# Later norm vectors: weights scaled on ScalarE, summed over k on GpSimd, partitions added once on TensorE

## The chip, the cores and the metric

The kernel runs on one core of one Trainium2 chip. The metric is device time in microseconds of one launch, the median of several runs. Besides, one execution was taken by the hardware profiler; its rows are what the prediction rests on. A core has five engines with a queue each: TensorE (PE in the rows, its weight loads PEld), VectorE (DVE), ScalarE (ACT), GpSimd (POOL) and SyncE (SP), which here issues the weight transfers.

## The reference

Two transformer layers on 512 tokens of width 1024, in float32. Each layer first makes six vectors of length 1024 out of one conditioning vector `c`; they scale, shift and gate the two halves of the layer. Cut to what matters:

```python
c_act = jax.nn.silu(c)                                  # [1, 1024]
for i in range(DEPTH):                                  # 2 layers
    mod = c_act @ ada_w[i] + ada_b[i]                   # [1, 6144], ada_w[i] is [1024, 6144]
    sh1, sc1, g1, sh2, sc2, g2 = jnp.split(mod[:, None, :], 6, axis=-1)
    h = _rmsnorm(x, norm_g[i, 0]) * (1.0 + sc1) + sh1
    mix = diff_attention(h, ...) if i % 2 == 0 else nsa_attention(h, ...)
    x = x + g1 * mix
    h = _rmsnorm(x, norm_g[i, 1]) * (1.0 + sc2) + sh2
    x = x + g2 * hier_moe(h, ...)                       # 32 experts, 2 of them for each token
return _rmsnorm(x, final_g)
```

## The kernel before

The product of `c_act` with `ada_w` (25 MB per layer) is done in blocks. Block (l, b) is two of the six vectors of layer l, 2048 columns of `ada_w`: b = 0 is sh1 and sc1, b = 1 is g1 and sh2, b = 2 is sc2 and g2. Block (0, 0) is needed at once and is made by `ada_first`; the other five, the later ones, by `ada_block`, a generator that is advanced in steps between other work.

A weight matrix has its 1024 rows laid out as 128 partitions by KC = 8 values of k. For each k, `ada_steps` multiplies the column `csil[:, k]` (silu of c, copied to 32 columns) with four groups of 512 columns, each into 32 partitions of one PSUM bank `acc`, so that the four land in four column groups of TensorE. The bank is added up over the eight k, then VectorE adds the bias (`nc.vector.tensor_tensor(row, acc, row, op=OP.add)`, line 243), the sc vectors get 1 + and the norm weight, and the four rows are stored to DRAM, from where later stages read them.

Weights stream through two units of 16 KB per partition, `ring[0]` and `ring[1]`, taken in turn by `unit()`. A block takes four units, two k each. Each unit is loaded in four pieces of 512 KB on SyncE's queue by `piece`, which lets a piece start only when the third one before it has landed and when its area of the ring has been read. The same two units also hold the weights of the projections (`w_in`, `w_out`), so blocks and projections follow one another there.

PSUM banks come from one pool with three names: four banks `mm` (projections, `ada` blocks, part of layer 1's scores), two `tr` (transposes), two `sc` (scores). A projection `dense` holds all four `mm` banks, one for each block of 128 rows, over its eight k; for each k, ScalarE and VectorE split 128x512 weights into two parts `wh` and `wl` (lines 369 and 370, four buffers each), and TensorE does three products for each row block.

The order of the work is written out by hand and then laid on the engines by the framework's scheduler, which takes instructions in the order of the program where they are ready:

```python
for w in "v0 h0 q1 a8 h1 h2 q2 a8 h3 v1 h4 q3 a8 h5".split():   # layer 0
```

Here q and v are projection units, h is an attention head, and a8 is eight steps, one whole block: (0,1), (0,2), (1,0). Behind a q unit come four rounds of evacuation: ScalarE copies the bank to `qkt`, GpSimd rotates it (`rope_to`, lines 324 to 330), TensorE transposes it, ScalarE and VectorE write it as two parts. Heads 6 and 7 and the output projection follow. In layer 1, `nsa_block` does two halves of eight scores for each of eight (group, row block) pairs and calls `do(ada_rest, 2)` once in each half, so blocks (1,1) and (1,2) are done in the first four pairs. In each half, GpSimd scales the first of four heads' weights `Pt`, VectorE the other three (line 1254), before TensorE transposes them.

Of the kernel before, what the change touches and what calls it, by code (L numbers as in the profile page):

```python
# [11 lines left out]
F32 = mybir.dt.float32  # L12
# [4 lines left out]
AF = mybir.ActivationFunctionType  # L17
OP = mybir.AluOpType
# [4 lines left out]
P = 128  # L23
# [3 lines left out]
KC = D // P  # L27
# [54 lines left out]
def tile_kernel(ctx, tc, x, c, positions, ada_w, ada_b, norm_g, final_g, diff_w_in, diff_w_out,  # L82
# [3 lines left out]
    nc = tc.nc  # L86
    pinned = set()

    def pin(i, engine):

        return tc.keep_in_program_order(i) if engine in pinned else i

    def mm(*a, **k):
        return pin(nc.tensor.matmul(*a, **k), "PE")  # L94
# [9 lines left out]
    cst = ctx.enter_context(tc.tile_pool(name="cst", bufs=1))  # L104
# [4 lines left out]
    def bank(tag):  # L109
        return ps.tile([P, 512], F32, name="b_" + tag, tag=tag, bufs={"mm": 4, "tr": 2, "sc": 2}[tag])  # L110
# [4 lines left out]
    def unit():  # L115
        t = ring[ring_at[0] % len(ring)]
        ring_at[0] += 1
        return t
# [3 lines left out]
    def piece(dst, src, paced=DEPTH_Q, after=None):  # L122


        i = nc.sync.dma_start(dst, src)
        if after is not None:
            tc.add_manual_dep(i.ins, after.ins.name,
                              mybir.DependencyInfo(mybir.DependencyClass.Sync, mybir.DependencyReason.DATA),
                              reason="behind the rows that the experts gather")
        if paced and len(stream) >= paced:  # L130
            tc.add_manual_dep(i.ins, stream[-paced].ins.name,
                              mybir.DependencyInfo(mybir.DependencyClass.Sync, mybir.DependencyReason.DATA),
                              reason="paced weight stream")
        stream.append(i)

    def wload(dst, src):
        h = dst.shape[-1] // 2
        if len(dst.shape) == 2:
            parts = [(dst[:, 0:h], src[:, 0:h]), (dst[:, h:], src[:, h:])]
        else:  # L140
            k = dst.shape[1] // 2
            parts = [(dst[:, 0:k], src[:, 0:k]), (dst[:, k:], src[:, k:])]
        for p in parts:
            piece(*p)
# [37 lines left out]

    ccol = cst.tile([P, KC], F32, name="ccol")
    nc.scalar.dma_start(ccol, c.rearrange("b (p k) -> (b p) k", k=KC))
    csil = cst.tile([P, KC], F32, name="csil")
    nc.scalar.activation(csil, ccol, AF.Silu)  # L186
    mod_d = [[dram.tile([4, 512], F32, name=f"mod{l}_{b}") for b in range(3)] for l in range(DEPTH)]

    def ada_steps(acc, l, b):

        for k in range(KC):
            if k % 2 == 0:
                w = unit()
                for kk in range(2):
                    wload(w[:, kk * 2048:(kk + 1) * 2048],
                          ada_w[l].rearrange("(p k) n -> p k n", k=KC)[:, k + kk, b * 2048:(b + 1) * 2048])
            lhsT = csil[:, k:k + 1].to_broadcast([P, 32])
            for g in range(4):
                c0 = k % 2 * 2048 + g * 512
                mm(acc[32 * g:32 * g + 32, :], lhsT, w[:, c0:c0 + 512], start=(k == 0), stop=(k == KC - 1),  # L200
                   skip_group_check=True)
            yield
# [24 lines left out]
        nc.vector.tensor_tensor(sh, cv[:, 0, :], bcol[:, 0, :], op=OP.add)  # L227
        return A, sh

    def ada_block(l, b):  # L230

        row = bcp.tile([P, D], F32, name="bc")
        row, gv = row[:, 0:512], row[:, 512:1024]
        lo = 64 if b == 0 else 0
        src = ada_b[l, b * 2048:(b + 1) * 2048]
        nc.scalar.dma_start(row, bass.AP(tensor=src.tensor, offset=src.offset, ap=[[512, 4], [0, 32], [1, 512]]))
        if b != 1:
            src = norm_g[l, 0 if b == 0 else 1]
            nc.scalar.dma_start(gv[lo:lo + 64], bass.AP(tensor=src.tensor, offset=src.offset,
                                                       ap=[[512, 2], [0, 32], [1, 512]]))  # L240
        acc = bank("mm")
        yield from ada_steps(acc, l, b)
        nc.vector.tensor_tensor(row, acc, row, op=OP.add)
        if b != 1:
            nc.vector.scalar_tensor_tensor(row[lo:lo + 64], row[lo:lo + 64], 1.0, gv[lo:lo + 64],
                                           op0=OP.add, op1=OP.mult)
        nc.scalar.dma_start(mod_d[l][b], row[0:P:32, :])
# [31 lines left out]
    with tc.tile_pool(name="rope", bufs=1) as rpool:  # L279
# [3 lines left out]
        kk = rpool.tile([P, NT, 8], F32, name="kk")  # L283
# [66 lines left out]
    def modulate(pool, tag, xk, k, Ac, shc, hi, lo):  # L350

        h = pool.tile([P, S], F32, name="h", tag=tag[0], bufs=tag[1])
        if k % 2:
            nc.scalar.activation(h, xk, AF.Identity, scale=Ac[:, k:k + 1], bias=shc[:, k:k + 1])
            nc.scalar.activation(hi[:, k, :], h, AF.Copy)
        else:
            nc.scalar.activation(hi[:, k, :], xk, AF.Identity, scale=Ac[:, k:k + 1], bias=shc[:, k:k + 1])
            nc.vector.tensor_scalar(h, xk, Ac[:, k:k + 1], shc[:, k:k + 1], op0=OP.mult, op1=OP.add)
        nc.vector.tensor_tensor(lo[:, k, :], h, hi[:, k, :].bitcast(F32), op=OP.subtract)
# [104 lines left out]
    m = main.enter_context(tc.tile_pool(name="main0", bufs=1))  # L464
    qkv_stack = ExitStack()
    qp = qkv_stack.enter_context(tc.tile_pool(name="qkv0", bufs=1, side="right"))
# [152 lines left out]
                    nc.vector.tensor_tensor(xs[:, t0 + u, qq], xs[:, t0 + u, qq], tmp, op=OP.add)  # L619

    qk_unit(0, lambda k: modulate(qp, ("wh", 4), xT[k // 4][:, k % 4, :], k, Ac, shc, hi, lo))
    ada0 = itertools.chain(ada_block(0, 1), ada_block(0, 2), ada_block(1, 0))
    for w in "v0 h0 q1 a8 h1 h2 q2 a8 h3 v1 h4 q3 a8 h5".split():
        {"v": v_unit, "q": qk_unit, "h": diff_head, "a": lambda n: do(ada0, n)}[w[0]](int(w[1:]))
    do(ada0)
# [382 lines left out]
    g = open_moe(0)  # L1008
# [14 lines left out]
    qp = qkv_stack.enter_context(tc.tile_pool(name="qkv1", bufs=1, side="right"))  # L1023
# [14 lines left out]
    w = unit().rearrange("p (k n) -> p k n", k=KC)  # L1038
# [6 lines left out]
    m = main.enter_context(tc.tile_pool(name="main1", bufs=1))  # L1045
# [73 lines left out]
    w = unit()[:, 0:KC * 304].rearrange("p (k n) -> p k n", k=KC)  # L1119
# [10 lines left out]
    b = bank("tr")  # L1130
# [26 lines left out]
    for cc in range(16):  # L1157
        for z, (blk, w1) in enumerate(rows):
            mm(hb[64 * z:64 * z + 64, 0:HID], blk[:, cc].rearrange("p g n -> p (g n)"), w1[cc // 8][:, cc % 8],
               start=(cc == 0), stop=(cc == 15), skip_group_check=True)  # L1160
# [7 lines left out]
    m1, m = m, main.enter_context(tc.tile_pool(name="main1b", bufs=1))  # L1168
# [6 lines left out]
    b = bank("tr")  # L1175
# [4 lines left out]
    b = bank("mm")  # L1180
# [12 lines left out]
    b = bank("mm")  # L1193
# [9 lines left out]
    def nsa_block(gi, i):  # L1203
# [65 lines left out]
        for st in range(2):  # L1269
            for hh in range(4):  # L1270
# [4 lines left out]

    ew = Experts(1, [("g", 0, 0), ("g", 0, 1), ("g", 2, 0), ("g", 1, 0), ("g", 1, 1), ("g", 2, 1), ("d", 0, 0), ("d", 1, 0), ("d", 2, 0),
                     ("d", 3, 0)])
    ada_rest = itertools.chain(ada_block(1, 1), ada_block(1, 2))
    w_o = nsa_w_out[0].rearrange("(g s h d) n -> g s d h n", g=2, s=2, h=4)

    def load_wo(w, q):
# [16 lines left out]
    g = open_moe(1)  # L1298
# [44 lines left out]
```

## Time and profile before

| | us |
|---|---|
| median of three runs | 1371.77 |
| lowest and highest | 1371.35, 1374.61 |
| the profiled execution | 1373.53 |
| its span, first to last instruction | 1371.7 |
| TensorE busy | 1267.9 |
| VectorE busy | 752.7 |
| ScalarE busy | 557.4 |
| GpSimd busy | 178.4 |

The profile gives the time in which an engine had an instruction in work as busy. Matmuls overlap one another in TensorE's pipeline, so its busy time is the time covered by at least one. A float32 matmul of two passes has two records. The granted clock is the share of TensorE's full clock of 2.4 GHz.

### The profile page before, as it was taken

The page shows a single profiled execution, that of the slowest core. Times are in us where ns is not written, and L with a number is a line of the kernel's source. Part 1 is how long each engine was busy: PE and PEld are TensorE (multiplying, and loading weights), DVE is VectorE, ACT ScalarE, POOL GpSimd, SP SyncE. Part 2 cuts the span into 40 slices and gives each one's busy share as a digit, 9 for nine tenths or more (in the row PEclk, how much of TensorE's full clock was granted, in tenths as well). Part 3 has the DMA queues.
Part 4 walks back from the last instruction along what each step waited for, and adds up shares of the span by engine and source line. Part 5 has one row for each costly group of instructions (what it writes and reads, how often), then busy time and mean ns, then how long its engine had stood idle before and what let it go on. Part 6 is the DMA issues. An engine that isn't in the chain of part 4 may idle for free.

```text
span 1371.7 us, 18259 instructions
## 1 busy us (share of the span) xinstructions
PE 1267.9 (92%) x6431; PEld 762.7 (56%) x6431; DVE 752.7 (55%) x1671; ACT 557.4 (41%) x1332; POOL 178.4 (13%) x304
## 2 busy tenths in 40 slices
PE   4899999989969999999799799999999599999995
PEld 0587668657734444444688554556558544444442
DVE  2444756586525555556654455657645426555557
ACT  2443644455423332222554444655644143332222
POOL 0021120212210000000142111112120200000001
PEclk7899999989969999999999899999999699999998
DMA  7722855486759999994432174510054579999971
GB/s 252 233 95 75 287 179 192 135 296 197 253 169 365 400 402 408 408 408 154 128 109 92 62 261 151 142 63 1 17 190 138 150 285 380 396 408 408 407 279 62
DMA packets 104607, 309.84 MB, mean 226 GB/s; under 512 B 13888, under 2 KB 27680, under 8 KB 104500
## 3 DMA queue, kind: packets, MB, share of 16 engines
q1 hardware_dynamic: 93920, 288.59, 58.3%
q0 software_dynamic: 6304, 12.96, 2.8%
q10 hardware_dynamic: 4276, 6.96, 1.7%
q8 instruction: 55, 0.90, 0.3%
q14 instruction: 52, 0.43, 0.1%
HBM read 310.52 MB, written 6.34 MB: 231 GB/s over the span
## 4 chain that ended last, share of the span: by engine, by line
PE 45%; DVE 2%; issue 2%; ACT 1%; DMA 1%; POOL 1%; ACTq 0%; POOLq 0%; DVEq 0%
PE b_mm L94 31%; PE b_sc L94 8%; PE b_tr L97 6%; DMA xg<-xr_d,toks 1%; DVE nm L397 0%; DVE xs L919 0%; DVE y L911 0%; ACT slot L398 0%; DVE yl L382 0%; DVE otmp L618 0%; ACT yh L381 0%; DVE slot L1254 0%; POOL rs L179 0%; DVE blk L1149 0%; ACTq L1129 0%
## 5 line engine op out<-in xcount | busy, mean ns | idle before, releaser
L94 PE MATMUL b_mm<-slot,xT 128*64 128x512 f32 x640 | 187.8, 608 | 2.3 <-ACT xT L868 2.0
L94 PE MATMUL b_mm<-ring,xT 128*64 128x512 f32 x384 | 126.6, 592 | 0.0
L94 PE MATMUL b_mm<-wh,h_hi 128*128 128x512 f32 (+1 forms) x320 | 116.5, 395 | 7.2 <-ACT wh L369 5.5
L94 PE MATMUL b_mm<-wl,h_hi 128*128 128x512 f32 (+1 forms) x320 | 122.2, 391 | 0.7 <-DVE wl L370 0.6
L94 PE MATMUL b_mm<-wh,h_lo 128*128 128x512 f32 (+1 forms) x320 | 120.5, 388 | 0.0
L94 PEld LDWEIGHTS b_mm<-slot,xT 128*64 128x64 f32 x640 | 60.0, 141 | 93.5 <-issue 86.4
L883 DVE TENSOR_TENSOR ac<-b_mm,sl 128x256 f32<-128x256 f32 x32 | 20.0, 625 | 159.8 <-ACT sl L881 159.8
L868 ACT ACTIVATE xT<-b_tr,col_sh,col_A 128x128 f32<-128x128 f32 x256 | 93.0, 468 | 2.5 <-PE b_tr L97 0.5
L919 DVE TENSOR_TENSOR xs<-xs,b_mm 128x512 f32<-128x512 f32 x128 | 86.4, 675 | 2.8 <-PE b_mm L94 2.8
L94 PE MATMUL b_mm<-ring,csil 128*32 128x512 f32 x384 | 78.6, 668 | 9.7 <-ACT csil L186 4.8
L919 DVE TENSOR_TENSOR xs<-xs,b_sc 128x512 f32<-128x512 f32 x128 | 86.5, 676 | 0.3 <-PE b_sc L94 0.3
L848 POOL DMA_INDIRECT xg<-xr_d,toks x32 | 32.4, 1012 | 358.7 <-DVE xn L855 321.4
L881 ACT ACTIVATE sl<-b_mm 128x256 f32<-128x256 f32 x32 | 12.3, 384 | 157.6 <-PE b_mm L94 147.9
L94 PE MATMUL b_sc<-slot,slot 128*128 128x128 f32 (+3 forms) x232 | 72.8, 389 | 3.8 <-ACT slot L398 1.3
L370 DVE TENSOR_TENSOR wl<-ring,wh 128x512 fp32r<-128x512 f32 (+1 forms) x80 | 53.2, 673 | 39.0 <-ACT wh L369 37.4
L1264 ACT ACTIVATE pT<-b_tr 128x512 f32<-128x512 f32 x80 | 47.4, 597 | 65.4 <-PE b_tr L97 64.8
L381 ACT ACTIVATE yh<-y 128x512 fp32r<-128x512 f32 x64 | 40.3, 630 | 78.5 <-DVE y L911 78.5
L94 PEld LDWEIGHTS b_mm<-wh,h_hi 128*128 128x128 f32 x320 | 60.3, 192 | 18.6 <-ACT wh L369 6.0
L94 PEld LDWEIGHTS b_mm<-ring,xT 128*64 128x64 f32 x384 | 39.9, 137 | 54.8 <-issue 54.8
L397 DVE TENSOR_REDUCE nm<-b_sc 128x1 f32<-128x128 f32 (+3 forms) x116 | 54.2, 482 | 27.2 <-PE b_sc L94 26.1
L369 ACT ACTIVATE wh<-ring 128x512 fp32r<-128x512 f32 (+1 forms) x80 | 48.4, 614 | 50.2 <-PE b_mm L94 36.7
L382 DVE TENSOR_TENSOR yl<-y,yh 128x512 fp32r<-128x512 f32 x64 | 44.3, 692 | 44.0 <-ACT yh L381 43.6
(307 smaller groups left out, 2648.8 us busy)
## 6 DMA issues: line engine op xcount, KB each, us to landing
ring<-in_ada_w_dram SPq DMA_DIRECT2D x96, 512.0 KB
slot<-in_moe_w_gate_dram SPq DMA_DIRECT2D x80, 512.0 KB
slot<-in_moe_w_up_dram SPq DMA_DIRECT2D x80, 512.0 KB
dn<-in_moe_w_down_dram SPq DMA_DIRECT2D x80, 512.0 KB
slot<-in_moe_w_down_dram SPq DMA_DIRECT2D x48, 512.0 KB
ring<-in_moe_w_gate_dram SPq DMA_DIRECT2D x48, 512.0 KB
ring<-in_moe_w_up_dram SPq DMA_DIRECT2D x48, 512.0 KB
ring<-in_diff_w_in_dram SPq DMA_DIRECT2D x24, 512.0 KB
```

The source lines that it names most:

```text
L94: return pin(nc.tensor.matmul(*a, **k), "PE")
L97: return pin(nc.tensor.transpose(*a), "PE")
L369: nc.scalar.activation(wh[:, :n], w[:, k, :], AF.Copy)
L370: nc.vector.tensor_tensor(wl[:, :n], w[:, k, :], wh[:, :n].bitcast(F32), op=OP.subtract)
L381: nc.scalar.activation(h_out, src, AF.Copy)
L382: nc.vector.tensor_tensor(l_out, src, h_out.bitcast(F32), op=OP.subtract)
L397: nc.vector.tensor_reduce(nm, b[:, :n], axis=AX.X, op=OP.max, negate=True)
L848: nc.gpsimd.indirect_dma_start(out=xg, out_offset=None, in_=xr_d[:, :], in_offset=bass.IndirectOffsetOnAxis(ap=tab[0][:, q:q + 1], axis=0) ...
L868: nc.scalar.activation(xT[:, k, :], b[:, kk * P:(kk + 1) * P], AF.Identity, scale=g.Ac[:, k:k + 1], bias=g.shc[:, k:k + 1])
L883: nc.vector.tensor_tensor(ac.rearrange("p (k t) -> p t k", k=2), hb[:, HID:512].rearrange("p (t k) -> p t k", k=2), sl.rearrange("p (t k) ...
L919: nc.vector.tensor_tensor(g.xs[:, t, zz], g.xs[:, t, zz], b, op=OP.add)
L1264: nc.scalar.activation(pT, b, AF.Copy)
```

## The change

For the five later blocks, each half of a block (1024 columns) is made by itself. A unit of the ring now holds four k of one half. ScalarE multiplies the 128x1024 weights of each k with the column `csil[:, k]`, in place, or for k = 0 into a new buffer `ada_sums` (one buffer, in the pool that is passed in). GpSimd adds the scaled weights of k = 1 to 7 to it. Then TensorE multiplies a block of ones, 128x32, with the sum's two groups of 512 columns, which adds the 128 partitions and puts the result into 32 partitions each; VectorE adds the bias to that half of the rows. A generator step is two k of one half, so a block still has eight. `ada_first` is left as it was.

```diff
+    ones_f = cst.tile([P, 32], F32, name="ones_f")
+    nc.gpsimd.memset(ones_f, 1.0)
...
-    def ada_block(l, b):
+    def ada_block(l, b, pool):
...
-        acc = bank("mm")
-        yield from ada_steps(acc, l, b)
-        nc.vector.tensor_tensor(row, acc, row, op=OP.add)
+
+        for h in range(2):
+            sums = pool.tile([P, 1024], F32, name="ada_sums", bufs=1)
+            c0 = b * 2048 + h * 1024
+            for k in range(KC):
+                if k % 4 == 0:
+                    w = unit().rearrange("p (k n) -> p k n", k=4)
+                    for kk in range(4):
+                        piece(w[:, kk], ada_w[l].rearrange("(p k) n -> p k n", k=KC)[:, k + kk, c0:c0 + 1024])
+                dst = sums if k == 0 else w[:, k % 4]
+                nc.scalar.activation(dst, w[:, k % 4], AF.Copy, scale=csil[:, k:k + 1])
+                if k:
+                    nc.gpsimd.tensor_tensor(sums, sums, dst, op=OP.add)
+                if k == KC - 1:
+                    acc = bank("mm")
+                    hh = slice(64 * h, 64 * h + 64)
+                    for g in range(2):
+                        mm(acc[64 * h + 32 * g:64 * h + 32 * g + 32, :], ones_f, sums[:, g * 512:(g + 1) * 512],
+                           start=True, stop=True, skip_group_check=True)
+                    nc.vector.tensor_tensor(row[hh], acc[hh], row[hh], op=OP.add)
+                if k % 2:
+                    yield
...
-    ada0 = itertools.chain(ada_block(0, 1), ada_block(0, 2), ada_block(1, 0))
+    ada0 = itertools.chain(ada_block(0, 1, qp), ada_block(0, 2, qp), ada_block(1, 0, qp))
...
-    ada_rest = itertools.chain(ada_block(1, 1), ada_block(1, 2))
+    ada_rest = itertools.chain(ada_block(1, 1, m), ada_block(1, 2, m))
```

## Rows read from the trace of the kernel before

**Rows 1.** The page's first part: busy us of each engine, share, instructions.

```profile
PE 1267.9 (92%) x6431; PEld 762.7 (56%) x6431; DVE 752.7 (55%) x1671; ACT 557.4 (41%) x1332; POOL 178.4 (13%) x304
```

**Rows 2.** Busy time by stage: length, engines (instructions), granted clock, DMA share, GB/s.

```profile
core 0: us, PE busy (x) PEld busy (x) DVE busy (x) ACT busy (x) POOL busy (x), PEclk, DMA share, GB/s
105.00:280.00 175.00, 172.94 (x960) 120.52 (x958) 98.69 (x241) 82.11 (x219) 25.94 (x53) 1.00 0.53 177
132.00:156.00 24.00, 22.80 (x145) 11.22 (x144) 16.86 (x43) 14.09 (x40) 7.18 (x15) 1.00 0.80 275
280.00:314.00 34.00, 25.50 (x141) 19.83 (x139) 27.50 (x86) 17.58 (x65) 3.40 (x4) 0.85 0.88 291
785.00:884.00 99.00, 98.95 (x571) 52.92 (x570) 60.36 (x187) 48.13 (x145) 15.35 (x14) 0.96 0.57 181
```

**Rows 3.** The same view for instructions on `csil` alone: PE, PEld, ACT busy.

```profile
105.00:280.00 175.00, 34.57 (x192) 6.11 (x192) 0.00 (x0) 1.00 0.53 177
...
785.00:884.00 99.00, 22.76 (x128) 4.30 (x128) 0.00 (x0) 0.96 0.57 181
```

**Rows 4.** Timeline of TensorE, first burst: start us, us, line, operation, out<-in, records.

```profile
133.34 3.64 PE L94 MATMUL b_mm<-ring,csil 128*32 128x512 f32 x32
...
148.92 0.60 PE L97 MATMUL b_tr<-ident,qkt 128*128 128x128 f32 x4
149.45 1.05 PE L94 MATMUL b_mm<-ring,csil 128*32 128x512 f32 x4
150.43 0.66 PE L97 MATMUL b_tr<-ident,qkt 128*128 128x128 f32 x4
...
152.60 0.30 PE L97 MATMUL b_tr<-ident,a 128*128 128x128 f32 x1
...
156.33 1.17 PE L94 MATMUL b_mm<-wh,h_hi 128*128 128x512 f32 x4
```

**Rows 5.** Timeline of VectorE, the same burst.

```profile
136.51 0.35 DVE L555 SCALAR_TENSOR_TENSOR a<-es,r 128x128 f32<-128x128 f32 x1
```

**Rows 6.** Groups of GpSimd by line and shape: busy us, mean ns, idle before.

```profile
L330 POOL TENSOR_TENSOR qkt<-rope_a,rope_b 128x256 f32<-128x256 f32 x24 | 17.8, 751 | 1.0
...
L324 POOL TENSOR_TENSOR rope_a<-qkt,rope_c 128x128 f32<-128x128 f32 x24 | 11.0, 460 | 179.6 <-ACT qkt L516 142.6 <-ACT qkt L1104 36.9
...
L1254 POOL TENSOR_SCALAR slot<-slot,r 128x512 f32<-128x512 f32 x4 | 8.1, 2027 | 12.7 <-DVE r L1252 10.1 <-ACT slot L398 2.5
...
L1254 POOL TENSOR_SCALAR Pt<-Pt,r 128x128 f32<-128x128 f32 x4 | 2.5, 615 | 36.9 <-PE b_mm L94 19.7 <-DVE r L1252 17.1
```

**Rows 7.** Groups of ScalarE by line and shape.

```profile
L868 ACT ACTIVATE xT<-b_tr,col_sh,col_A 128x128 f32<-128x128 f32 x256 | 93.0, 468 | 2.5 <-PE b_tr L97 0.5
...
L337 ACT ACTIVATE junk<-xs 128x1024 bf16<-128x1024 f32 x12 | 12.6, 1053 | 7.3 <-DVE xs L619 5.0 <-DVE xs L919 2.0
...
L381 ACT ACTIVATE slot<-b_tr 128x128 fp32r<-128x128 f32 x16 | 4.5, 278 | 9.4 <-PE b_tr L97 7.8 <-DVE slot L382 1.4
```

**Rows 8.** Groups of VectorE by line and shape.

```profile
L386 DVE TENSOR_TENSOR slot<-b_tr,slot 64x512 fp32r<-64x512 f32 x32 | 21.9, 693 | 35.2 <-ACT slot L385 34.8
```

**Rows 9.** Timeline of VectorE and GpSimd, at four places.

```profile
141.01 0.56 DVE L553 SCALAR_TENSOR_TENSOR r<-r,l,nlam 128x1 f32<-128x1 f32 x1
...
140.83 0.73 POOL L330 TENSOR_TENSOR qkt<-rope_a,rope_b 128x256 f32<-128x256 f32 x1
...
171.11 0.22 DVE L553 SCALAR_TENSOR_TENSOR r<-r,l,nlam 128x1 f32<-128x1 f32 x1
...
872.42 1.72 DVE L1254 TENSOR_SCALAR slot<-slot,r 128x512 f32<-128x512 f32 x3
...
872.58 2.02 POOL L1254 TENSOR_SCALAR slot<-slot,r 128x512 f32<-128x512 f32 x1 [6.32 <-DVE r L1252]
...
878.93 1.27 DVE L1254 TENSOR_SCALAR Pt<-Pt,r 128x512 f32<-128x512 f32 x3
```

## The prediction

> **What bounds the kernel now.** The page's first part comes first: TensorE (PE) is busy 1267.9 of 1371.7 us, VectorE (DVE) 752.7, ScalarE (ACT) 557.4, GpSimd (POOL) 178.4 [rows 1]. So TensorE is the fullest engine and GpSimd nearly empty. But these are means over stages. The five later vector blocks run in two of them only: three in layer 0's first attention stage (105 to 280 us), two in the first half of layer 1's attention (785 to 884 us). In both, the stage table shows TensorE at 172.94 of 175 and 98.95 of 99 us, at full granted clock or close to it (1.00 and 0.96), and no other engine over 61% [rows 2]. The matmuls on c take 34.57 and 22.76 us of this, 192 and 128 records [rows 3]. They are the whole of what the change takes from TensorE: 57.3 us. The profiled execution took 1373.53 us, its span is 1371.7; what lies around the span, 1.8 us, does not change. The median of the runs shown, 1371.77, is 1.76 below this execution.
>
> Busy is not the same as bound, and the next view, TensorE's order of work, shows why. In layer 0 the blocks run in three bursts of about 34.57/3 = 11.5 us, each after a projection unit's products, while that unit's results are evacuated: the burst of block (0,1) opens with 32 records at 133.34 us and goes on in groups of four, each between two groups of transposes of `qkt`, until 152 [rows 4]. Those transposes come only as fast as ScalarE and GpSimd rotate the rows. Head 1's first row `a` is computed at 136.51 [rows 5], but its transposes stand at 152.60, behind the last of `qkt` [rows 4]: the banks of one name are handed out in program order. So in a burst the matmuls on c partly fill time in which TensorE's other work is not ready. In layer 1 there are no such holes to see.
>
> **The change, part by part.**
>
> *Removed from TensorE*: 57.3 us, 320 records (five blocks of eight k by four, two records each). *Added*: per half block two 32-column products in neighbouring column groups, four records. The old groups of four records are the same shape; one takes 1.05 us and holds TensorE about 1 us [rows 4]. Ten halves: 10 us. If all of it lay on the path: 57.3 - 10 = 47 us saved.
>
> *Added on ScalarE*: 16 scalings of 128x1024 per block, 80 in all, none of which exist now. The nearest 128x1024 instruction takes 1.05 us, from SBUF with a constant scale. A column operand costs extra: 128x128 with scale and bias columns takes 468 ns, a copy of the same shape 278, so 95 ns for one column [rows 7]. I take 1.15 us (from below 1.05, from above 1.05 + 0.19 = 1.24). That is 18.4 us per block.
>
> *Added on GpSimd*: 14 additions of 128x1024 per block, 70 in all. Additions of 128x128 and 128x256 take 460 (a product) and 751 ns [rows 6]: 2.27 ns per element, so 0.75 + 768 x 2.27 = 2.5 us; I take 2.4, since the 128x256 one is strided. From above: the scaling of 128x512 takes 2.03 us and that of 128x128 0.615 [rows 6], 3.7 ns per element, so 3.9 us for 1024. From below: 2.0, the 128x512 duration. It is nearer to the additions, which are the same operation. At 2.4 a block costs 34 us of GpSimd.
>
> *DVE*: ten evacuating additions of 64 partitions in place of five of 128. One of 64x512 takes 0.69 us [rows 8], so 5 x 0.69 = 3.5 us more, spread over stages where VectorE has 40% free; no cost as long as that stays. *DMA*: the same 16 pieces per block over the same four ring units; only their order changes. Each piece now waits until GpSimd, not TensorE, has read the area it overwrites. The small write of ones at the start is off every path.
>
> *Layer 0.* The first two ring units were there when the burst opened (32 records are four k, two units [rows 4]), so the first half's sum can be made during the projection before it. The single `ada_sums` buffer is free once TensorE has added the first half's partitions, at about 134.3. The second half then needs seven additions behind the rotations that GpSimd does there anyway (7.18 us [rows 2]): 134.3 + 16.8 + 7.2 = 158.3, plus 1 us of product and 0.7 of addition: 160. Until then the next unit lacks its fourth PSUM bank; in the trace its products start at 156.33 [rows 4]. It can run ahead with three of its four row blocks for four k (four `wh` buffers): 36 products, at 1.17 us for four [rows 4] up to 10.5 us. So the 4 us of lateness are covered, and TensorE has something to do in the holes that c's matmuls leave. But the burst itself hardly gets shorter, for ScalarE in it goes from 14.09 of 24 us [rows 2] to 14.09 + 8 x 1.15 = 23.3 with one half's scalings. I therefore count what runs ahead, not what is removed: of the 11.5 - 2 = 9.5 us per burst, 4 us each in the first two (between nothing and 9.5). In the third, what follows is heads 5 to 7, where TensorE is at 25.50 of 34 us and VectorE at 27.50 [rows 2]: nothing gained. Layer 0: -8 us (0 to -28.7).
>
> *Layer 1.* Of 99 us TensorE would need 98.95 - 22.76 + 4 = 80.2; ScalarE 48.13 + 32 x 1.15 = 84.9; GpSimd 15.35 + 28 x 2.4 = 82.6 [rows 2, 3]. Three engines end up level, so ScalarE caps the gain at 14 us. All three hang in one chain (a scaled `Pt` on GpSimd feeds transposes, an Exp on ScalarE feeds it) and each now waits behind an instruction of 1.15 or 2.4 us, so I take half: -7 us (0 to -14). In favour: the block's PSUM bank is held only at the end of each half, so scores have three banks of the name instead of two for most of the time.
>
> *VectorE and GpSimd at once.* In one place a small VectorE instruction on SBUF, 0.22 us elsewhere, took 0.56 and ended with the GpSimd addition beside it (140.83 + 0.73 = 141.56). In another, three scalings took 1.72 us beside a GpSimd one against 1.27 alone [rows 9]: up to 0.45 us each. At 0.45 us for each addition layer 1's VectorE goes to 60.36 + 28 x 0.45 = 73 of 99 us and layer 0's to 98.69 + 42 x 0.45 = 118 of 175: free. The bounds are nothing and the addition's whole 2.4 us.
>
> The Trainium skill ("SBUF — State Buffer", section "SBUF: two separate sides") says that the port pair VectorE and GpSimd share is locked exclusively for a whole instruction and that the other engine blocks. By that rule an addition could hold VectorE for its whole length, which is the fourth rival below; the first of the two rows agrees, the second does not: there 0.45 us were lost beside an instruction of 2.02.
>
> **Sum.** -8 - 7 = -15 us against 1373.53, so 1358.5; less 1.76 to compare with the median: 1357.
>
> **Rivals.** (1) *TensorE is the limit throughout.* For it: the 100% in both stages. Against it: the holes between the transposes, ScalarE's 23.3 of 24 us. Then -28.7 in layer 0 and -14 in layer 1: 1329.
>
> (2) *The matmuls on c were hidden anyway.* They fill holes in layer 0; in layer 1 the level of the three engines eats the rest. Then the time stays: 1372.
>
> (3) *GpSimd becomes the limit, slower.* Place: additions ahead of the rotations and of the `Pt` scalings, and late sums that hold the PSUM bank and the ring. It decides from (99 - 15.35)/28 = 3.0 us per addition in layer 1. At 3.3 us, a tenth past that point and within the bound of 3.9: 15.35 + 92.4 = 107.8, +9 us; in layer 0 the second half ends at 134.3 + 23.1 + 7.2 + 1.7 = 166.3, 10 us late and just covered, so about +2 in each of two bursts. +13: 1385. Against it: the plain additions' rate.
>
> (4) *VectorE waits for whole additions, slower.* It decides where the mean wait passes (99 - 60.36)/28 = 1.4 us in layer 1. At 1.75 us, midway between half and all of an addition: 60.36 + 49 = 109, +10; layer 0: 98.69 + 73.5 = 172 of 175, nothing gained: 1382.
>
> **Chances.** Forecast 0.43, (1) 0.10, (2) 0.17, (3) 0.20, (4) 0.10. Runs here differ by about 0.3% (4 us) without a change. Faster by more: 0.10, 0.40 of the forecast's 0.43, 0.04 of (2): 0.54. Within: 0.15. Slower: (3), (4) and the last of (2): 0.31. The forecast's own range is 1344 to 1369. The range over all must reach into (1) and past (3) and (4): 1336 to 1388 leaves about 0.05 below and 0.1 above.
>
> **What would show it.** Right: c's matmuls fall from 384 records to 64; 40 records of ones by `ada_sums` at about 1 us per half; 70 GpSimd additions with a mean of 2.0 to 3.0 us; 80 scalings near 1.15; the projection after each burst starting within 5 us of its old distance to the burst, with some products of three row blocks ahead; layer 1's first half shorter by some 7 us, ScalarE near 90% there. Wrong: additions over 3 us, VectorE instructions of over 1 us beside them, TensorE idle behind `bc` or GpSimd in the bursts, or a second scoring group that waits for a PSUM bank.

## The result, and the profile after

The changed kernel takes 1456.51 us (median, 1455.10 to 1457.09) against 1371.8: slower by 84.7 us, a ratio of 1.0615 with a 95% interval of 1.0597 to 1.0633. The forecast was 1357.0, the range 1336 to 1388. The profiled execution took 1455.1 us, its span is 1453.3, the mean granted clock 0.911 (0.954 before).

The page's first part, answering to [rows 1]:

```profile
PE 1270.1 (87%) x6151; PEld 780.3 (54%) x6151; DVE 837.5 (58%) x1676; ACT 637.2 (44%) x1412; POOL 347.0 (24%) x375
```

ScalarE and GpSimd grew as forecast. VectorE grew by 84.8 us, although it was given 3.5 us more to do, and TensorE, with 320 records less on `csil`, is as busy as before, at a lower mean clock.

Stage windows, answering to [rows 2] (132 to 156 is the window of the first burst before; then the three bursts of layer 0 as they lie now, and layer 1's first half, which took 99 us before):

```profile
132.00:156.00 24.00, 13.87 (x56) 8.94 (x54) 14.66 (x26) 15.59 (x33) 15.64 (x17) 0.60 0.48 156
137.00:182.00 45.00, 24.48 (x87) 15.10 (x88) 35.18 (x56) 23.39 (x57) 25.58 (x24) 0.55 0.42 139
213.00:258.00 45.00, 26.76 (x109) 17.68 (x110) 35.83 (x63) 25.43 (x65) 25.63 (x24) 0.63 0.46 141
318.00:366.00 48.00, 34.35 (x143) 25.11 (x142) 38.93 (x91) 26.88 (x78) 26.43 (x27) 0.58 0.61 204
850.00:972.00 122.00, 105.33 (x496) 64.71 (x497) 97.37 (x205) 78.82 (x187) 79.83 (x42) 0.83 0.48 137
```

A burst of 24 us became one of 45. In it TensorE is busy for half the time and at a granted clock of 0.55, so mostly at its 1.2 GHz level, where [rows 2] had 1.00. VectorE is now the fullest engine there, 35.18 of 45 us.

Groups by line and shape, answering to [rows 3, 6, 7]:

```profile
L255 POOL TENSOR_TENSOR ada_sums<-ada_sums,ring 128x1024 f32<-128x1024 f32 x70 | 169.1, 2416 | 132.0 <-ACT ring L253 70.4 <-ACT ada_sums L253 37.8 <-DMA ring<-in_ada_w_dram 15.0
L253 ACT ACTIVATE ring<-ring,csil 128x1024 f32<-128x1024 f32 x70 | 80.4, 1152 | 71.8 <-DMA ring<-in_ada_w_dram 68.1 <-DVE nm L418 3.2
L391 DVE TENSOR_TENSOR wl<-ring,wh 128x512 fp32r<-128x512 f32 x72 | 71.7, 1006 | 35.8 <-ACT wh L390 35.4
L94 PE MATMUL b_mm<-ring,csil 128*32 128x512 f32 x64 | 19.9, 822 | 9.1 <-ACT csil L188 4.9 <-DMA ring<-in_ada_w_dram 4.0
L574 DVE SCALAR_TENSOR_TENSOR r<-r,l,nlam 128x1 f32<-128x1 f32 x32 | 20.6, 644 | 0.8
L94 PE MATMUL b_mm<-ada_sums,ones_f 128*32 128x512 f32 x40 | 15.2, 849 | 5.9 <-issue 5.9
```

An addition takes 2.416 us (2.4 forecast), a scaling 1.152 (1.15). What the forecast did not foresee, and only the fourth rival did, stands in VectorE's lines: `wl` took 692 ns before, now 1006, and the 128x1 `r` 265, now 644. The lines of before:

```profile
L370 DVE TENSOR_TENSOR wl<-ring,wh 128x512 fp32r<-128x512 f32 x72 | 49.4, 692 | 36.1 <-ACT wh L369 34.7 <-DMA ring<-in_ada_w_dram 0.9
L553 DVE SCALAR_TENSOR_TENSOR r<-r,l,nlam 128x1 f32<-128x1 f32 x32 | 8.5, 265 | 0.7
```

The timeline of VectorE in the first burst, answering to [rows 5, 9]:

```profile
144.17 1.83 DVE L574 SCALAR_TENSOR_TENSOR r<-r,l,nlam 128x1 f32<-128x1 f32 x1
145.93 3.47 DVE L599 SCALAR_TENSOR_TENSOR o_n<-o_n,rs,subg 128x128 f32<-128x128 f32 x4
...
150.16 1.88 DVE L576 SCALAR_TENSOR_TENSOR a<-es,r 128x128 f32<-128x128 f32 x1
...
160.41 9.34 DVE L391 TENSOR_TENSOR wl<-ring,wh 128x512 fp32r<-128x512 f32 x4
```

That of GpSimd beside it:

```profile
143.63 4.84 POOL L255 TENSOR_TENSOR ada_sums<-ada_sums,ring 128x1024 f32<-128x1024 f32 x2 [0.16 <-ACT ada_sums L253]
...
149.54 2.35 POOL L255 TENSOR_TENSOR ada_sums<-ada_sums,ring 128x1024 f32<-128x1024 f32 x1
...
160.91 8.29 POOL L255 TENSOR_TENSOR ada_sums<-ada_sums,ring 128x1024 f32<-128x1024 f32 x3
```

And that of TensorE, answering to [rows 4]:

```profile
137.48 1.92 PE L94 MATMUL b_mm<-ada_sums,ones_f 128*32 128x512 f32 x4 [1.84 <-issue]
...
150.27 1.09 PE L97 MATMUL b_tr<-ident,qkt 128*128 128x128 f32 x4 [3.60 <-DVE slot L407]
...
171.16 2.13 PE L97 MATMUL b_tr<-ident,qkt 128*128 128x128 f32 x8 [9.14 <-DVE slot L407]
...
179.79 1.78 PE L94 MATMUL b_mm<-ada_sums,ones_f 128*32 128x512 f32 x4
181.50 0.50 PE L94 MATMUL b_mm<-wh,h_hi 128*128 128x512 f32 x1
```

Its waits before transposes, from the view of waits of the whole run (us in total, times, longest):

```profile
PE b_tr L97 <- DVE slot L407: 30.7, 11, 9.1
PE b_tr L97 <- POOL qkt L351: 2.7, 2, 1.9
```

Read them together. Four `wl`, 2.8 us of work, take 9.34 us and end at 169.75, just after the three additions beside them (169.20). The evacuation of `b_tr` on line 407 stands behind them on VectorE, so TensorE's next transposes wait 9.14 us. `a` ends at 152.04, the addition beside it at 151.89. The first product of the next projection comes at 181.50, behind the second half's ones; none ran ahead.

### The profile page after: what moved, and what is told of

Read it like the earlier page. It is cut to its first block, busy times and chain, and to the rows that moved or that the text cites. A ratio compares the mean times of both kernels' runs of the same rounds, so it can differ in the third digit from the quotient of the medians.

```text
span 1453.3 us, 17845 instructions
## 1 busy us (share of the span) xinstructions
PE 1270.1 (87%) x6151; PEld 780.3 (54%) x6151; DVE 837.5 (58%) x1676; ACT 637.2 (44%) x1412; POOL 347.0 (24%) x375
## 5 line engine op out<-in xcount | busy, mean ns | idle before, releaser
L255 POOL TENSOR_TENSOR ada_sums<-ada_sums,ring 128x1024 f32<-128x1024 f32 x70 | 169.1, 2416 | 132.0 <-ACT ring L253 70.4
L253 ACT ACTIVATE ring<-ring,csil 128x1024 f32<-128x1024 f32 x70 | 80.4, 1152 | 71.8 <-DMA ring<-in_ada_w_dram 68.1
L94 PE MATMUL b_sc<-slot,slot 128*128 128x128 f32 (+3 forms) x232 | 87.8, 454 | 24.5 <-ACT es L419 14.6
L391 DVE TENSOR_TENSOR wl<-ring,wh 128x512 fp32r<-128x512 f32 (+1 forms) x80 | 75.4, 954 | 38.8 <-ACT wh L390 38.2
L94 PEld LDWEIGHTS b_sc<-slot,slot 128*128 128x128 f32 x232 | 54.1, 244 | 38.8 <-ACT es L419 24.3
L97 PE MATMUL b_tr<-ident,qkt 128*128 128x128 f32 x224 | 42.2, 329 | 35.7 <-DVE slot L407 27.4
```

The lines of the kernel that those rows point to most:

```text
L97: return pin(nc.tensor.transpose(*a), "PE")
L253: nc.scalar.activation(dst, w[:, k % 4], AF.Copy, scale=csil[:, k:k + 1])
L255: nc.gpsimd.tensor_tensor(sums, sums, dst, op=OP.add)
L391: nc.vector.tensor_tensor(wl[:, :n], w[:, k, :], wh[:, :n].bitcast(F32), op=OP.subtract)
```

## The experiments

The first theory (A) was that VectorE is held for whole additions, which was the fourth rival. Its rival (B) was that GpSimd's own load and late sums do it, the third. A third theory (C), that the scalings wait for weights at the head of ScalarE's queue, stands in the expectations from the second run on. In the table every run is set against the kernel before on the same chip (1368.4 to 1373.2 us from chip to chip). "First gather" is the start of the experts' first gather of layer 0, so a mark of all that layer 0's attention lost; the kernel before has 382.1. The runs e8, e10 and e12 stand in the text alone.

| run | us | against before | instruction on GpSimd, mean us | VectorE busy | first gather |
|---|---|---|---|---|---|
| changed kernel | 1456.5 | +84.7 | addition, 2.42 | 837.5 | 446.7 |
| e1 quarter additions | 1433.7 | +62.2 | four of 0.785 | 805.1 | 433.1 |
| e2 GpSimd writes only | 1404.9 | +33.4 | three memsets, 2.4 | 779.8 | 406.5 |
| e3 additions on VectorE | 1413.0 | +41.5 | none | 826.7 | 413.0 |
| e4 no scalings | - | - | addition, 2.44 | - | 421.9 |
| e5 neither | 1361.4 | -10.3 | none | 755.9 | 382.4 |
| e6 short scalings | 1435.8 | +64.2 | addition, 2.42 | 842.2 | 430.2 |
| e7 scalings only | 1392.1 | +20.5 | none | 756.6 | 400.1 |
| e9 both loaded | 1427.4 | +54.2 | three memsets, 2.4 | 848.3 | 418.2 |
| e11 one source | 1384.8 | +11.5 | one source, 1.77 | 764.9 | 400.4 |
| e13 one source, long | 1437.6 | +68.4 | one source, 2.81 | 781.3 | 423.3 |
| e14 short scalings alone | 1379.4 | +10.2 | none | 757.6 | 396.2 |
| e15 half-length additions | 1386.7 | +17.5 | addition, 1.30 | 783.1 | 400.4 |
| e16 one source, equal | 1415.4 | +46.9 | one source, 2.39 | 775.7 | 411.3 |
| e17 two sources, off the chain | 1424.6 | +56.2 | in place, 1.92 | 793.6 | 416.7 |
| e18 one source, off the chain | 1424.8 | +56.4 | in place, 2.38 | 766.3 | 418.3 |

### Each addition in four

```diff
-                    nc.gpsimd.tensor_tensor(sums, sums, dst, op=OP.add)
+                    for q in range(4):   # 256 columns each
+                        nc.gpsimd.tensor_tensor(sums[:, q], sums[:, q], dst[:, q], op=OP.add)
```

> Each GpSimd addition of 128x1024 is made as four of 128x256, so 280 additions in place of 70. By the nearest row one takes about 0.75 us, so GpSimd's added work grows from 169 to about 210 us. Theory A (VectorE's instructions with SBUF operands wait until the GpSimd addition beside them ends): a wait is at most 0.75 us in place of 2.4, so the four wl of a projection unit that took 9.34 us take under 6, VectorE's busy time falls from 837 to about 800, and the time to 1400 to 1430 us. Theory B (GpSimd is late by itself: its queue holds the rotations, the PSUM bank, the sum's buffer and the ring): 40 us more of GpSimd work, so no gain or a loss: 1455 to 1490 us.

It took 1433.72 us, just outside what A gave. `wl` fell to 789 ns, although GpSimd now spends 3.1 us on an addition instead of 2.4. So shorter instructions on GpSimd help VectorE even where GpSimd has more to do, but most of the loss stays.

### GpSimd only writes

```diff
-                    nc.gpsimd.tensor_tensor(sums, sums, dst, op=OP.add)
+                    nc.gpsimd.memset(dst, 0.0)
+                    nc.gpsimd.memset(sums, 0.0)
+                    nc.gpsimd.memset(sums[:, 0:512], 0.0)
```

> In place of each GpSimd addition stand three GpSimd writes of zeros (1024, 1024 and 512 columns, over the scaled weights and the sum), which read nothing and by the memset rows (944 ns for 1025) take about 2.4 us together; what is left out is the sum, so the later vectors are only their biases. All waits on GpSimd, the ring, the sum's buffer and the PSUM bank stay. Theory A: VectorE's two-operand instructions are not held by an instruction that reads nothing: wl back at about 0.69 us mean, the time down to 1350 to 1390. Theory B: GpSimd is as occupied as with the additions, so the time stays at 1440 or more. Theory C (ScalarE's scalings, which wait for weights at the head of its queue): stays too, since the scalings are there.

1404.89 us, between the two: 33 us stay, which A did not name. `wl` is back at 714 ns. (The memsets of the sums do not wait for the scaled weights, so this run also has a shorter chain: the ones of the first burst's second half start at 162.47, in the changed kernel at 179.79. The run e16 below keeps the chain.)

### The additions on VectorE

```diff
-                    nc.gpsimd.tensor_tensor(sums, sums, dst, op=OP.add)
+                    nc.vector.tensor_tensor(sums, sums, dst, op=OP.add)
```

> The 70 additions of 128x1024 are made by VectorE, about 1.2 us each (1279 ns for the 128x1024 instruction with two tensors). Theory A: VectorE's 85 us of waiting are replaced by some 85 us of work, but no small instruction waits 2 us and GpSimd's rotations are free, so the time falls to 1390 to 1430. Theory B: GpSimd has nothing of it any more, so the time falls below that of before, 1340 to 1370. Theory C: stays above 1430.

1413.03 us, as A had it; B missed. An addition takes 1.227 us there. VectorE is about as busy as in the changed kernel (826.7 and 837.5 us) and the time is 43 us shorter: work in VectorE's own order seems to cost less than the same time spent held. GpSimd is free of the additions here too, so this run alone does not part the two; e9 below loads GpSimd again.

### Without the scalings

```diff
-                nc.scalar.activation(dst, w[:, k % 4], AF.Copy, scale=csil[:, k:k + 1])
+                if k == 0:
+                    nc.scalar.activation(dst, w[:, k % 4], AF.Copy, scale=csil[:, k:k + 1])
```

> The scalings of k = 1 to 7 on ScalarE are left out (70 of 80), so the sum is that of unscaled weights for these k; GpSimd's additions are all there. Theory A: VectorE still waits, at most 20 us are gained: 1435 to 1455. Theory B: the same, or a little more since additions start earlier. Theory C: ScalarE no longer waits for weights (68 us in the trace after): 1375 to 1400.

The unscaled vectors route the tokens otherwise: the experts gather 144 times instead of 32 and the run takes 10,690.81 us, so only what lies ahead of them can be read. The first gather is at 421.9 against 446.7: the scalings cost some 25 of the 65 us of layer 0. A and B had not counted on that. C had, but its 1375 to 1400 can't be held against this run's time.

### Neither scalings nor additions

```diff
-                nc.scalar.activation(dst, w[:, k % 4], AF.Copy, scale=csil[:, k:k + 1])
-                if k:
-                    nc.gpsimd.tensor_tensor(sums, sums, dst, op=OP.add)
+                if k == 0:
+                    nc.gpsimd.memset(sums, 0.0)
```

> Left out: all 80 scalings and all 70 additions; the sums are a buffer of zeros written once per half block, multiplied by ones that are set to zero, so the later norm vectors hold their biases alone. The weights are still loaded, the 40 records of ones and the evacuating additions remain. Theory A (the 85 us come from the work added to the other engines: VectorE held by additions, ScalarE loaded with scalings; each about additive): 1335 to 1372, layer 0's first gather of the experts at 382 us or before (kernel before: 382.1). Theory B (what is left without the additions comes from TensorE itself: without the matmuls on c it idles in the bursts and falls to its lower clock, or the sums' hand-over comes late): 1385 or more, the gather at 395 or later.

1361.35 us: theory A. This is what the relief of TensorE is worth with nothing set against it, 10 us. By the marks none of it is in layer 0: the first gather of the run without both, timeline of the tile `xg` (ns least, median, most; first and last start):

```profile
L868 POOL DMA_INDIRECT xg<-xr_d,toks x32: 988/988/1174, 382.4 to 1266.3; - x32
```

382.4 against 382.1. TensorE's next products did start earlier. Here are ScalarE's first split of the weights of unit v1, that of the output projection, and the last row of a head that VectorE writes, first for the kernel before and then for this run:

```profile
203.81 1.14 ACT L369 ACTIVATE wh<-ring 128x512 fp32r<-128x512 f32 x2
279.43 0.62 ACT L604 ACTIVATE wh<-ring 128x512 fp32r<-128x512 f32 x1
314.73 0.35 DVE L566 TENSOR_SCALAR o_n<-b_tr,r 128x128 f32<-128x128 f32 x1
...
179.07 0.63 ACT L389 ACTIVATE wh<-ring 128x512 fp32r<-128x512 f32 x1 [8.27 <-DMA ring<-in_diff_w_in_dram]
263.89 0.63 ACT L624 ACTIVATE wh<-ring 128x512 fp32r<-128x512 f32 x1 [7.21 <-DMA ring<-in_diff_w_out_dram]
314.56 0.34 DVE L586 TENSOR_SCALAR o_n<-b_tr,r 128x128 f32<-128x128 f32 x1
```

The projections start 24.7 and 15.5 us earlier, although ScalarE waits 8.27 and 7.21 us for their weights. But v1's first bank is copied out only 7.2 us earlier (220.83, before 228.03), and the last head ends where it did. So the lead goes into waits for weights and into the heads; which of the two decides is not shown. Two stretches of this run:

```profile
175.00:190.00 15.00, 10.25 (x37) 8.14 (x38) 7.55 (x22) 5.64 (x16) 1.02 (x1) 0.66 0.90 300
250.00:280.00 30.00, 19.61 (x100) 13.97 (x99) 18.60 (x46) 14.86 (x41) 10.21 (x20) 0.74 0.81 265
```

TensorE is busy for two thirds at clocks of 0.66 and 0.74, where the whole stage before was at 1.00 [rows 2], and yet layer 0 takes no more time. In layer 1, from the first to the last copy `pT`, 206.7 us pass in this run and 218.1 before: all the gain, 11.4 us, is there.

### Short scalings, with the additions

```diff
-                nc.scalar.activation(dst, w[:, k % 4], AF.Copy, scale=csil[:, k:k + 1])
+                dst = w[:, k % 4]
+                nc.scalar.activation(dst[:, 0:32], dst[:, 0:32], AF.Copy, scale=csil[:, k:k + 1])
```

> Each scaling works on 32 of the 1024 columns (so the vectors' values are left out: the ones are zero), but still waits for its weights at the head of ScalarE's queue; the additions are whole. The scalings cost some 25 us in layer 0 (first gather at 446.7 with both, 421.9 with additions alone). Theory A1 (it is ScalarE's time, 1.15 us each): gather at 415 to 428, total 1415 to 1435. Theory A2 (it is ScalarE's wait for weights in its in-order queue): gather at 440 to 450, total 1440 to 1460.

1435.81 us and the gather at 430.2: between A1 and A2, so ScalarE's time and its waits both cost.

### Scalings alone

```diff
-                if k:
-                    nc.gpsimd.tensor_tensor(sums, sums, dst, op=OP.add)
```

> Left out: the 70 additions, with nothing on GpSimd in their place; the scalings are whole and in place; the ones are zero, so the vectors hold their biases alone. Theory A (what is left without the additions is the scalings): like the run with GpSimd writes only, gather at 400 to 408, total 1390 to 1406. Rival C (GpSimd's own occupancy in that run, ahead of its rotations, was part of the 33 us left): gather at 395 or before, total 1385 or less.

1392.14 us, theory A. The scalings cost 31 us beside the run with neither. But it is 13 us below the run with GpSimd writes only, so the memsets had a price of their own, as rival C says.

### The kernel before, with matmuls of four k together

```diff
-            for g in range(4): ...
-            yield
+            held.append((k, w))
+            if k % 4 == 3 or first:
+                for kk, ww in held: ...   # 16 matmuls in a row
+                held = []
+            yield
```

> The kernel before, with the matmuls on c of four k issued together (16 records in one group in place of four groups of 4) for the later blocks; nothing is left out. In the trace of before 32 such records together took 3.64 us, 0.455 per four, a group of 8 took 1.70, one of 4 about 1.05. If TensorE's time in the bursts and in layer 1 is on the path, up to 3 us per block: 1357 to 1366. If these matmuls fill holes anyway: 1368 to 1376.

1374.10 us, a ratio of 1.0018 (1.0000 to 1.0037): the same. In the bursts of layer 0 the records came out in groups of four as before, with other work between them; in layer 1 they fell from 22.76 [rows 3] to 19.73 us, and those 3 us did not show in the time.

### Both engines loaded, VectorE not held by additions

```diff
-                    nc.gpsimd.tensor_tensor(sums, sums, dst, op=OP.add)
+                    nc.vector.tensor_tensor(sums, sums, dst, op=OP.add)
+                    nc.gpsimd.memset(dst, 0.0)   # twice, and 512 columns once more
```

> The additions on VectorE, and beside each three memsets of the scaled piece on GpSimd (some 2.4 us), so both engines are loaded while GpSimd reads nothing; the ones are zero, so the vectors hold their biases alone. If loads of the two engines only add up: 1404.9 (memsets alone) + 1413.0 (additions on VectorE alone) - 1392.1 (scalings only) = 1426, 1415 to 1435. If it is two loaded engines in one chain that made the changed kernel slow, and not that GpSimd's additions hold VectorE: 1445 or more.

1427.42 us: the loads of the two engines add up, and some 30 us of the changed kernel are not explained by them, although VectorE is 11 us busier here.

### Layer 1 by VectorE alone

```diff
+                nc.vector.scalar_tensor_tensor(sums, w[:, k % 4], csil[:, k:k + 1], sums, op0=OP.mult, op1=OP.add)
```

> Layer 0's three blocks as before; layer 1's two blocks by VectorE alone, each piece scaled and added in one instruction with two operands (about 1.25 us, 32 of them), ones on TensorE; nothing left out. Theory A (TensorE's relief in layer 1 is worth 11 to 12 us, as in the run with neither; VectorE has room and costs some 8 to 11, as the additions on it did): 1364 to 1374. Rival (waits for weights and 40 us of work in VectorE's queue cost more than the relief): 1378 or more.

1383.53 us, a ratio of 1.0082 (1.0065 to 1.0099): the rival, and no version that beats the kernel before. 28 such instructions of 1.271 us, with their waits for weights, cost more than the relief gives.

### One source in place of two

```diff
-                    nc.gpsimd.tensor_tensor(sums, sums, dst, op=OP.add)
+                    nc.gpsimd.tensor_scalar(sums[:, 0:608], dst[:, 0:608], 1.0, None, op0=OP.mult)
```

> Each addition replaced by a GpSimd instruction with one source (a multiplication by 1 of 608 columns of the scaled piece into the sums, about 2.4 us); the sums are so left out, the ones are zero. Theory A' (it is the second source of the addition that holds VectorE; the small price of 0.45 us in the forecast came from a one-source instruction): near the run with GpSimd writes only, 1398 to 1415, VectorE busy 765 to 785, wl near 0.72 us. Rival (any long GpSimd instruction that reads SBUF holds VectorE, and the small price was a chance of timing): 1440 to 1460, VectorE busy over 820.

1384.76 us, VectorE busy 764.9, `wl` 716 ns: theory A', even below its ranges, and 9 us less over its kernel before than scalings alone, which no run explains. But the instruction took 1.77 us, not 2.4, so length and sources are not told apart yet.

### Layer 1 alone as changed

```diff
-    ada0 = itertools.chain(ada_block(0, 1, qp), ada_block(0, 2, qp), ada_block(1, 0, qp))
+    ada0 = itertools.chain(ada_block(0, 1), ada_block(0, 2), ada_block(1, 0))   # as before
```

> Layer 0's three blocks as before; layer 1's two blocks as changed (ScalarE scales, GpSimd adds); nothing left out. Shares by stage, read off the traces of before and after: layer 0 +66 us, layer 1 +17. Theory A (the stages lose each by themselves): 1384 to 1394. Rival (layer 1 lost because layer 0 had put its transfers or its order late): 1366 to 1378.

1382.73 us, 9.5 above its chip's kernel before, just below A's range and above the rival's. Layer 1 loses by itself, some 10 us rather than 17.

### One source, longer; short scalings alone; half the columns

```diff
+                    nc.gpsimd.tensor_scalar(sums, dst, 1.0, None, op0=OP.mult)
```

> Each addition replaced by a multiplication by 1 of all 1024 columns of the scaled piece into the sums: one source, about 2.9 us by 1.77 us for 608 columns, so longer than the addition's 2.42; the sums are so left out, the ones are zero. If one source does not hold VectorE and GpSimd has room: 1380 to 1405, VectorE busy under 785. If the one-source run was fast because its instruction was 0.65 us shorter than the addition: 1425 or more.

1437.59 us: theory A' falls as the whole of it. VectorE is busy for 781.3 us, hardly held, and 68 us are lost. TensorE's waits behind GpSimd's rotations show up in the view of waits, where the changed kernel had 30.7 behind VectorE and 2.7 behind GpSimd:

```profile
PE b_tr L97 <- POOL qkt L351: 14.4, 7, 2.9
PE b_tr L97 <- DVE slot L407: 13.1, 9, 3.0
```

The scalings of 32 columns, without additions:

> No additions, and each scaling on 32 of 1024 columns (it still waits for its weights at the head of ScalarE's queue); the ones are zero. With neither: 1361.4; with whole scalings alone: 1392.1. If the 31 us are ScalarE's time (some 0.9 us more for each of 80): 1361 to 1372. If they are the waits for weights in its queue: 1382 to 1393.

1379.40 us, 10.2 above before: about two thirds of the scalings' 31 us are there already with instructions of 0.32 us. ScalarE waits for weights at the head of its queue, 94.0 us in all:

```profile
L256 ACT ACTIVATE ring<-ring,csil 128x32 f32<-128x32 f32 x80 | 25.5, 323 | 95.3 <-DMA ring<-in_ada_w_dram 94.0 <-DVE Pt L1276 1.3
```

The additions of 512 columns (the slices `[:, 0:512]` of both):

> As many additions, each on 512 of the 1024 columns (about 1.3 us; the sums of the other half are left out, the ones are zero); scalings whole. If VectorE is held for the additions' length, half of the 64 us between scalings only (1392.1) and the changed kernel (1456.5): 1415 to 1432, VectorE busy near 797. If the loss is a fixed price for each addition: 1445 or more.

1386.66 us, no worse than scalings alone. VectorE is busy for 783.1 us, not 797. The price in time is neither fixed nor in proportion to the length: at 1.30 us it is nothing.

### The four cells at equal length

```diff
+                    nc.gpsimd.tensor_scalar(sums[:, 0:864], dst[:, 0:864], 1.0, None, op0=OP.mult)
```

> Each addition replaced by a multiplication by 1 of 864 columns of the scaled piece into the sums: one source, and by 1.77 us for 608 columns and 2.83 for 1024 as long as the addition (2.42 us). It stays in the chain of the sums, so the sums come as late as additions make them, with little hold on VectorE; the sums are left out, the ones are zero. If late sums and GpSimd's queue are the cause: 1440 or more. If the hold on VectorE is: 1385 to 1400. If both, by a straight line between the two one-source runs: near 1417 (1407 to 1430).

1415.36 us, what "both" gave (1417). This instruction takes 2.389 us and the addition 2.416, and each sum waits for seven of them. Without additions VectorE was busy for 756.6 us, here for 775.7, in the changed kernel for 837.5. Two sources instead of one cost 38 us more. VectorE and GpSimd in the first burst of this run:

```profile
154.74 9.99 POOL L255 TENSOR_SCALAR ada_sums<-ring 128x864 f32<-128x864 f32 x4
154.88 1.32 DVE L391 TENSOR_TENSOR wl<-ring,wh 128x512 fp32r<-128x512 f32 x1 [0.33 <-ACT wh L390]
...
156.32 2.59 DVE L391 TENSOR_TENSOR wl<-ring,wh 128x512 fp32r<-128x512 f32 x3
```

The four `wl` that took 9.34 us beside additions take 3.91 beside a row of one-source instructions.

Outside the chain of the sums, with two sources (`tensor_tensor(dst, dst, dst)`) and with one (864 columns of `dst` in place):

> The addition adds each scaled piece to itself in place: two sources and the same length, but the sums are the first scaled piece alone and wait for no addition (the sums are left out, the ones are zero). The hold on VectorE remains, late sums are gone. If the hold is the cause: 1445 or more. If late sums are: 1385 to 1405. If both: about 1431 (1420 to 1440).

> Both: one source (864 columns, as long as an addition), in place on the scaled piece, outside the chain of the sums (left out; the ones are zero). What is left is GpSimd's time alone. With scalings only: 1392.1. If GpSimd's time by itself costs nothing: 1385 to 1397; if its queue delays the rotations by itself: 1405 or more.

1424.63 and 1424.78 us. By their ranges the first reads "both" and the second "its queue delays the rotations by itself". But they settle nothing about the chain: without it the second half's ones are issued at 144.65 and 142.44, ahead of the last two of the four rounds of rotations instead of behind all four, so the order of the whole burst is another; and the in-place addition took 1.92 us and held VectorE for 37 us in all, not 81. They show that GpSimd's time costs also where no sum waits for it, with e18 even 9 us above e16. Whether it costs by the rotations, by the sums or by the ring was not parted: for a piece of the ring that GpSimd still had to read, SyncE waited 59.3 us from 60 to 450 us in the changed kernel, 47.4 in e16 and 0.3 in e18.

## Why the prediction was wrong

Put in one row, each step against the kernel before of its own chip: relief of TensorE -10.3 (e5), ScalarE waiting and short instructions +20.5 (e14), the rest of the scalings' length +10.3 (e7), GpSimd's time with late sums and a small hold on VectorE +26.4 (e16), two sources in place of one +37.8. The sum is 84.7. Single runs stand behind each, so a step is good to some 5 us; another order of the steps would share them otherwise: with the additions in place the scalings' length costs 20.5 (e6), not 10.3.

The forecast and its two slower rivals, +13 and +10 us, all weighed added work against the free share of a stage. Most of the loss, 64.6 of 84.7 us to the first gather, came in layer 0, whose bursts have VectorE busy for 35 of 45 us, and it came from three engines together.

*Removed and added.* The records are as forecast, 320 fewer on `csil`, 40 of ones. The latter took 15.2 us, not 10: in layer 0 they stand in stretches at a clock of 0.55 to 0.63, and the 24 records there took 10.4 of the 15.2. (The bound of -28.7 for layer 0 should be three times 9.5, -28.5.)

*Durations on ScalarE and GpSimd*: right to two hundredths of a us.

*"VectorE and GpSimd at once"*: the step that failed most: it priced the hold at 0.45 us for each addition and called it free. Its 0.45 us came from a GpSimd scaling [rows 9], an instruction with one source, and VectorE had begun 0.16 us before it (872.42 and 872.58). For one source that size is not too small: e16 has VectorE 19.1 us busier than e7, 0.27 us for each of 70. The change issues additions with two sources in SBUF, and for them VectorE's excess is 84.8 - 3.5 = 81.3 us, 1.16 each. The other row of [rows 9] did show an addition, a short one, ending together with the held instruction; it was the nearer one in form. The rule of the Trainium skill ("SBUF — State Buffer", section "SBUF: two separate sides"), a lock for the whole instruction, agrees with the additions here (9.34 us for four `wl` beside 8.29 of additions) and not with the one-source form (2.59 us for three).

*The fourth rival* had the mechanism. Its point, a mean wait of 1.4 us, was worked out from layer 1's share of VectorE; 1.16 was enough. Between e16 and the changed kernel the first gather moves by 35.4 us: the hold costs in layer 0's bursts, where VectorE stands in the chain of each transpose.

*The third rival* is real too, and its point of 3.0 us, also from layer 1's share, was too high. One-source instructions of 1.77, 2.39 and 2.81 us cost 11.5, 46.9 and 68.4 us. From 1.77 to 2.39 GpSimd has 70 x 0.62 = 43 us more to do and the time grows by 35, four fifths of it. With scalings alone the price is 20.5, so by the same line, an estimate, it begins to grow at 1.77 + 0.62 x 9/35 = 1.9 us. At 2.39 us GpSimd is busy for 345.5 us of 1413.6; a share of the span told nothing about it.

*Layer 0, -8 us*: measured nothing, before any cost (382.4 against 382.1). With nothing added the next unit does run ahead, as forecast, but the lead is gone by the last head (314.56 against 314.73). What the forecast said of the third burst, that the heads behind it gain nothing, held for all three. In the changed kernel nothing ran ahead: no product of the next unit came before the second half's ones (179.79, then 181.50). So the lateness that the forecast thought covered was not: the seventh addition ends at 169.20, forecast 158.3, and the ones come at 179.79, behind TensorE's own late transposes, forecast 160.

*Layer 1, -7 us*: the relief was there, the gain was not. With nothing added it is 11.4 us, inside the 0 to -14; as changed, layer 1 alone loses 9.5 us (e12). ScalarE did not cap it: the first half was to have three engines level at 80 to 85 of 99 us, and took 122, with ScalarE busy for 78.82 of them and TensorE, the fullest, for 105.33.

*ScalarE* was priced as a cap alone. It cost 31 us, two thirds of it with hardly any length: an instruction that waits for weights at the head of its queue can hold up the copies and Exps behind it (68.1 us of such waits in the changed kernel). How much of the 20.5 us is these waits and how much the 25.5 us of short instructions themselves was not parted.

## What to carry to other kernels

Work moved to an emptier engine is paid in the bursts where that engine stands in the chain of each step, so weigh it against the slack of the burst and not against the span. What an engine is relieved of counts only where that engine ends last: layer 0 was relieved of 34.57 us of matmuls and its mark moved by 0.3. Take the price of GpSimd beside VectorE from an instruction of the same form: a long addition with two sources in SBUF is a pause for VectorE, one with a single source is much less of one (1.16 and 0.27 us). A moved instruction that waits for a transfer brings its wait to the queue that it joins.

## What the hardware showed unexpectedly

A one-element VectorE instruction took 1.83 us beside a GpSimd addition of 2.42 (0.22 at other places [rows 9]). The hold depends on the form of the GpSimd instruction, also at equal length: beside the run with scalings alone VectorE is busy 81 us longer with two tiles added (2.42 us each), 19 with one source (2.39), 37 with a tile added to itself (1.92) and 27 with half tiles added (1.30). Memsets did not hold `wl` (714 ns), but other instructions: VectorE was 23 us busier than with scalings alone, and the 128x2 `l` took 315 ns on average, with scalings alone 190. TensorE, idle for 28 to 46% of each burst, was granted 0.55 to 0.63 there, where it had 1.00 with the matmuls on c in between. In e5 stretches at 0.66 and 0.74 left layer 0 as long as before; what the clock cost in the changed kernel was not tried separately.
